# Softmax sums and output tiles of two attention branches: from VectorE and ScalarE to GpSimd

## The chip, the cores and the metric

The kernel runs on one core of one Trainium2 chip. The metric is the device time of one execution in microseconds (us), taken as the median of several runs. The engines are named as in the profile: PE is TensorE (matmul), PEld its weight loads, DVE is VectorE, ACT is ScalarE, POOL is GpSimd, SP is SyncE, which here only issues DMAs.

## The reference, cut to what matters

One layer over 1024 tokens and 256 context tokens, width 1024. Two attention branches of 8 heads (2 key/value heads, head width 64) run on the same input; then they are merged, and a feed-forward layer with a convolution follows. What the change touches is the softmax of the two branches:

```python
def _sink_softmax(scores, sink):                 # first branch (A): window of 128, and the context
    m = jnp.maximum(jnp.max(scores, axis=-1, keepdims=True), sink)
    e = jnp.exp(scores - m)
    return e / (jnp.sum(e, axis=-1, keepdims=True) + jnp.exp(sink - m))
...
p = jax.nn.softmax(_gqa_scores(q_blk, k_all), axis=-1)   # second branch (B): all tokens, and the context
```

## The kernel before, in words

The attention part works in 32 units, in this order: 16 of the first branch (`br` = 0), then 16 of the second (`br` = 1). A unit `br_i_g` is one block `i` of 128 queries and one group `g` of four heads. In the trace the first branch's units run from about 335 to 470 us, the second's to about 760. Names in the trace carry the unit: `sm_4_0` is the tile sm of block 4, group 0 (both branches use the same numbers; the order of time tells them apart).

A unit goes through these steps, and steps of neighbouring units run beside each other:

- `qprep`, two units ahead: POOL casts the unit's queries into `qs` and subtracts to get the low parts (L83 and L86 on `qs`); PE transposes them into `qtr` (four transposes, L483); ACT copies the result, and two DMAs swap its halves. `qs` has one buffer.
- `lat`, once for each head: PE computes scores into `s` (L493, L494, a mask matmul L528), DVE takes their negated maximum into `nm` while it copies them (L538), ACT takes the exponential into `p` and the row sum into `sm` (L505). In the second branch `cxp` does the context's columns first, with sums in `smc` and maxima in `other`.
- `norm`: the tile `f` (128 queries x 4 heads) is a difference of maxima or of maximum and sink; ACT takes its exponential, and it is added to the row sums `sm`. In the second branch POOL also scales the context's `p` by `f`.
- `value_steps`, for the unit before: PE transposes `p` into `ptr` (L614), ACT casts to `pth` (L623), DVE subtracts to `ptl` (L624). For one of the five key tiles in the first branch (two of ten in the second) ACT copies to `prw`, and POOL makes `pth` and `ptl` (pooled tiles). PE multiplies both with the values into `av` (L635, L636).
- `rows`: PE transposes `sm` into `str` (L577), the reciprocal row goes to `rb` by a DMA through memory, which spreads it over all partitions.
- `out_step`: ACT copies `av` to `avs`, POOL copies its upper half to `up`, two adds make the output tile `ot` (L647), POOL multiplies it by `rb` (L650) and splits it into the high and low parts `O` (L83, L86).

All this is written without an order between the engines. A scheduler sets the order of instructions on each engine when the program is built, by its own estimate of what each takes; on the chip each engine's instructions then start in that order, each when what it needs is there. So an edit in one unit can move many instructions of other steps. POOL's queue holds a few more things: in the second branch it casts the weights of the first branch's output product (`hwb`, `lwb`), and it issues the DMAs that add up weight tiles in memory (`sd`).

Of the kernel before, what the change touches and what calls it, by code (L numbers as in the profile page):

```python
# [10 lines left out]
ALU = mybir.AluOpType  # L11
AX = mybir.AxisListType

P = 128
# [54 lines left out]
def layer_kernel(  # L69
# [6 lines left out]
    nc = tc.nc  # L76
    PSUM = bass.MemoryType.PSUM

    def split(src, hi, lo, hi_eng, lo_eng):
        if hi_eng is nc.scalar:  # L80
            nc.scalar.copy(hi, src)  # L81
        elif hi_eng is nc.gpsimd:
            nc.gpsimd.tensor_scalar(out=hi, in0=src, scalar1=1.0, scalar2=0.0, op0=ALU.mult, op1=ALU.add)  # L83
        else:
            hi_eng.tensor_copy(hi, src)
        lo_eng.tensor_tensor(out=lo, in0=src, in1=hi.bitcast(F32), op=ALU.subtract)  # L86
# [8 lines left out]
    def ctile(shape, dt, name):  # L95
        return const.tile(shape, dt, tag=name, name=name)
# [7 lines left out]
    sinkb = ctile([P, 8], F32, "sinkb")  # L104
# [358 lines left out]
    class Unit:  # L463
# [94 lines left out]
        def norm(self):  # L558
            hc = slice(self.g * 4, self.g * 4 + 4)
            f = small(f"f_{self.id}", (P, 4))  # L560
            if self.br:
                nc.vector.tensor_tensor(out=f, in0=self.nm, in1=self.other, op=ALU.subtract)
                nc.scalar.activation(f, f, AF.Exp)
                nc.gpsimd.tensor_tensor(out=self.smc, in0=self.smc, in1=f, op=ALU.mult)
                nc.gpsimd.tensor_tensor(out=self.sm, in0=self.sm, in1=self.smc, op=ALU.add)
                for h in range(4):
                    p = self.pc[h, 1]
                    nc.gpsimd.tensor_scalar(out=p, in0=p, scalar1=f[:, h:h + 1], scalar2=0.0, op0=ALU.mult, op1=ALU.add)
            else:
                nc.vector.tensor_tensor(out=f, in0=self.nm, in1=sinkb[:, hc], op=ALU.add)  # L570
                nc.scalar.activation(f, f, AF.Exp)
                nc.vector.tensor_tensor(out=self.sm, in0=self.sm, in1=f, op=ALU.add)
                nc.vector.reciprocal(self.sm, self.sm)

        def rows(self):
            tr = pt_tile(f"str{self.id}")
            nc.tensor.transpose(tr[0:4, 0:P], self.sm, ident)  # L577
            self.rb = att.tile([P, 2, P], F32, tag="rb", name=f"rb{self.id}", bufs=2)
            row = self.rb[0:4, 0]
            if self.br:  # L580
                nc.vector.reciprocal(row, tr[0:4, 0:P])
            else:
                nc.scalar.copy(row, tr[0:4, 0:P])
            dn = dpool.tile([4, P], F32, tag=f"dn{self.id}", name=f"dn{self.id}")
            tokens.append(f"dn{self.id}")
            nc.sync.dma_start(dn, row)
            for a in range(2):
                nc.sync.dma_start(self.rb[a * HD:(a + 1) * HD],
                                  dn.rearrange("(b a) q -> a b q", a=2)[a].partition_broadcast(HD))
# [15 lines left out]
        def value_steps(self):  # L605
            nm, kt = self.id, self.kt
            vh = self.br * 2 + self.g
            last = self.id == f"1_{NT - 1}_1"
            parts = {}

            def tr_step(n):
                tr = pt_tile(f"ptr{nm}_{n}")
                for h in range(4):
                    nc.tensor.transpose(tr[:, h * P:(h + 1) * P], self.pslice(h, n), ident)  # L614
                hi = att.tile([P, 512], R32, tag="pth", name=f"pth{nm}_{n}", bufs=4)
                lo = att.tile([P, 512], R32, tag="ptl", name=f"ptl{nm}_{n}", bufs=4)
                pooled = n in POOL_LO[self.br] and not last
                if pooled:
                    rw = att.tile([P, 512], F32, tag="ptr", name=f"prw{nm}_{n}", bufs=2)
                    nc.scalar.copy(rw, tr)  # L620
                    split(rw, hi, lo, nc.gpsimd, nc.gpsimd)
                else:
                    nc.scalar.copy(hi, tr)  # L623
                    nc.vector.tensor_tensor(out=lo, in0=tr, in1=hi.bitcast(F32), op=ALU.subtract)  # L624
                parts[n] = hi, lo
                return pooled

            def av_step(n):
                first = self.left == len(kt)
                self.left -= 1  # L630
                if first:
                    self.av = ps2.tile([P, 512], F32, tag="av", name=f"av{nm}")
                hi, lo = parts.pop(n)
                v = VT[kt[n] // 2][:, kt[n] % 2, vh]
                nc.tensor.matmul(self.av, v, hi, start=first, stop=False)  # L635
                nc.tensor.matmul(self.av, v, lo, start=False, stop=self.left == 0)  # L636

            def out_step():
                av = self.av
                avs = att.tile([P, 512], F32, tag="ptr", name=f"avs{nm}", bufs=2)  # L640
                nc.scalar.copy(avs, av)  # L641
                up = att.tile([HD, 512], F32, tag="up", name=f"up{nm}", bufs=1)
                nc.gpsimd.tensor_scalar(out=up, in0=avs[HD:P], scalar1=1.0, scalar2=0.0, op0=ALU.mult, op1=ALU.add)
                ot = att.tile([P, 2, P], F32, tag="ot", name=f"ot{nm}", bufs=1)
                oe = nc.gpsimd if self.br and not last else nc.vector
                for h in range(2):
                    oe.tensor_tensor(out=ot[h * HD:(h + 1) * HD],  # L647
                                     in0=avs[0:HD].rearrange("p (a b q) -> p a b q", b=2, q=P)[:, :, h],
                                     in1=up.rearrange("p (a b q) -> p a b q", b=2, q=P)[:, :, h], op=ALU.add)
                nc.gpsimd.tensor_tensor(out=ot, in0=ot, in1=self.rb, op=ALU.mult)  # L650
                hf = self.i // 4
                qs = slice((self.i % 4) * P, (self.i % 4 + 1) * P)
                split(ot, otile(self.br, hf, 0, self.g)[:, :, qs], otile(self.br, hf, 1, self.g)[:, :, qs],
                      nc.gpsimd, nc.gpsimd)

            def step(ns):
                pooled = [tr_step(n) for n in ns]
                for n, pl in zip(ns, pooled):
                    clk[0] += 1
                    avq.append((self, n, clk[0] + LAG[self.br] + (PLAG[self.br] if pl else 0)))  # L660
                    av_issue()

            self.left = len(kt)
            self.av_step, self.out_step = av_step, out_step
            g = 1 + self.br
            steps = [lambda n=n: step(range(n, n + g)) for n in range(0, len(kt), g)]
            steps.insert(3 if self.br else 2 if self.i else len(steps), self.rows)
            return steps
# [155 lines left out]
    for n, (gi, k) in enumerate(order):  # L824
# [8 lines left out]
        if gi == "g":  # L833
            for hf in (0, 1):
                last = gate(k, hf)
# [50 lines left out]
    def otile(br, hf, hl, g):  # L886
        key = br, hf, hl, g
        if key not in O:
            O[key] = opool.tile([P, 2, HALF], R32, tag="O", name="O%d%d%d%d" % key, bufs=12)
        return O[key]  # L890
# [4 lines left out]
    def pt_tile(name, dt=F32):  # L895
        return ps2.tile([P, 512], dt, tag="pt", name=name, bufs=3)
# [10 lines left out]
    def small(name, shape):  # L907
        return att.tile(list(shape), F32, tag=name.split("_")[0], name=name,
                        bufs=4)
# [4 lines left out]
    def av_issue(flush=False):  # L914
        while avq:
            u = avq[0][0]
            c = [e for e in avq if e[0] is u and (flush or e[2] <= clk[0])]
            if not c:
                return
            e = min(c, key=lambda e: e[2])  # L920
            avq.remove(e)
            u.av_step(e[1])
            if u.left == 0:
                u.out_step()
# [1000 lines left out]
```

## Time and profile before

| what | before |
|---|---|
| median of 3 runs | 1564.17 us (1563.13 to 1565.62) |
| the profiled execution | 1565.22 us, of which 1563.4 us span |
| busy PE / DVE / ACT / POOL | 1531.6 / 1187.6 / 808.6 / 782.2 us |
| granted clock of TensorE, mean | 0.995 |

The span runs from the first to the last instruction; what the time has beyond it lies around the program. A share of busy time is a mean over stages with different limits, so the stages are looked at one by one. A row of the order of time reads: start, duration, engine, line, operation, tiles out<-in, shapes, count, and in brackets how long the engine stood idle before and what ended that.

### The profile page before, as it was taken

Reading aid. Unit: us, or ns where it says so; the run is one execution under the profiler, and the core shown is the slowest. Engines: PE = TensorE matmul, PEld = TensorE weight load, DVE = VectorE, ACT = ScalarE, POOL = GpSimd, SP = SyncE. Lnnn points to the kernel's source line nnn. Section 1 sums busy time; section 2 is a strip of 40 time slices with the busy share of each in tenths; the row PEclk is TensorE's granted clock in tenths of the full one; section 3 lists DMA queues with packets and bytes.
Section 4 is the critical chain, followed back from the end, with each engine's and each line's share of the span. In section 5 each row is a group of like instructions: output and inputs, shape, how many; then the busy total and the mean of one; then the engine's idle time right before and its main releaser. Section 6 shows DMA issues by size and latency. Waiting matters only on the chain.

```text
span 1563.4 us, 22286 instructions
## 1 busy us (share of the span) xinstructions
PE 1531.6 (98%) x7804; PEld 1282.2 (82%) x7804; DVE 1187.6 (76%) x1714; ACT 808.6 (52%) x1431; POOL 782.2 (50%) x795
## 2 busy tenths in 40 slices
PE   9999999999999999999999999999999999999997
PEld 7888888888877877877888997888888888888887
DVE  6677976548887777777774788888888888657884
ACT  5322223358887777777431673544444444435552
POOL 0356422526666777776332455666677764121121
PEclk9999999999999999999999999999999999999998
DMA  9776662322235666631550223233334446996721
GB/s 371 267 239 239 207 245 92 106 84 66 65 116 137 150 149 151 148 80 35 180 184 16 98 79 120 81 112 115 120 102 114 113 117 191 363 265 212 251 103 55
DMA packets 113105, 232.11 MB, mean 148 GB/s; under 512 B 13056, under 2 KB 27904, under 8 KB 112896
## 3 DMA queue, kind: packets, MB, share of 16 engines
q1 hardware_dynamic: 97760, 201.82, 38.4%
q0 software_dynamic: 10400, 20.19, 8.3%
q10 hardware_dynamic: 4832, 8.68, 1.5%
q8 instruction: 61, 1.00, 0.3%
q14 instruction: 52, 0.43, 0.1%
HBM read 179.45 MB, written 65.86 MB: 157 GB/s over the span
## 4 chain that ended last, share of the span: by engine, by line
PE 54%; DVE 3%; ACT 1%; issue 1%; POOL 0%; DVEq 0%; ACTq 0%
PE p L89 4%; PE p L90 4%; PE p L91 4%; PE b L89 2%; PE b L91 2%; PE b L90 2%; PE c L89 2%; PE c L91 2%; PE d L91 2%; PE d L89 2%; PE c L90 2%; PE d L90 2%; PE a L91 2%; PE a L89 2%; PE a L90 2%; PE y L91 2%
## 5 line engine op out<-in xcount | busy, mean ns | idle before, releaser
L624 DVE TENSOR_TENSOR ptl<-ptr,pth 128x512 fp32r<-128x512 f32 x190 | 126.2, 682 | 32.6 <-ACT pth L623 32.2
L623 ACT CAST pth<-ptr 128x512 fp32r<-128x512 f32 x190 | 108.0, 593 | 54.0 <-PE ptr L614 32.6
L86 DVE TENSOR_TENSOR ld<-rd,hd 128x1024 fp32r<-128x1024 f32 x77 | 94.9, 1249 | 50.2 <-ACT hd L81 48.1
L505 ACT ACTIVATE p<-p,nm 128x1024 f32<-128x1024 f32 (+2 forms) x128 | 125.9, 985 | 4.5 <-DVE p L538 4.3
L614 PE MATMUL ptr<-ident,p 128*128 128x128 f32 x816 | 122.4, 277 | 4.4 <-DVE ptl L624 3.2
L81 ACT CAST hd<-rd 128x1024 fp32r<-128x1024 f32 x77 | 79.5, 1050 | 81.1 <-PE p L91 55.1
L614 PEld LDWEIGHTS ptr<-ident,p 128*128 128x128 f32 x816 | 94.1, 141 | 25.6 <-DVE ptl L624 7.9
L86 POOL TENSOR_TENSOR wlg<-wg,whg 128x512 fp32r<-128x512 f32 x32 | 47.7, 1500 | 123.3 <-ACT whg L81 123.3
L635 PE MATMUL av<-pth,VT 128*128 128x512 f32 x236 | 104.6, 443 | 2.1 <-ACT avs L641 1.5
L89 PE MATMUL p<-hd 128*128 128x512 f32 x264 | 103.2, 391 | 0.0
L91 PE MATMUL p<-hd,ld 128*128 128x512 f32 x264 | 102.7, 389 | 0.0
L90 PE MATMUL p<-ld,hd 128*128 128x512 f32 x264 | 102.7, 389 | 0.0
L636 PE MATMUL av<-ptl,VT 128*128 128x512 f32 x236 | 98.1, 416 | 2.7 <-POOL ptl L86 2.7
L89 PE MATMUL g<-hh,whg 128*128 128x512 f32 x256 | 99.9, 390 | 0.0
L91 PE MATMUL g<-hh,wlg 128*128 128x512 f32 x256 | 99.7, 389 | 0.0
L90 PE MATMUL g<-hl,whg 128*128 128x512 f32 x256 | 99.6, 389 | 0.0
L538 DVE TENSOR_SCALAR_CACHE_REDUCE p<-s,cvt,nmc 128x1024 f32<-128x1024 f32 x64 | 83.2, 1316 | 8.8 <-PE s L494 7.7
L493 PE MATMUL s<-KL,q 128*128 128x512 f32 (+2 forms) x192 | 75.6, 394 | 5.3 <-ACT p_x L505 2.8
L787 ACT ACTIVATE sg<-g,bgc 128x512 f32<-128x512 f32 x32 | 22.0, 686 | 96.1 <-PE g L91 96.1
L494 PE MATMUL s<-KL,q 128*128 128x512 f32 (+2 forms) x192 | 71.6, 373 | 0.0
L81 ACT CAST wS<-s 128x512 fp32r<-128x512 f32 x76 | 45.3, 620 | 46.4 <-POOL s L1227 45.7
L81 ACT CAST wA<-ru 128x512 fp32r<-128x512 f32 x57 | 35.5, 623 | 62.4 <-PE d L91 33.8
(436 smaller groups left out, 5015.2 us busy)
## 6 DMA issues: line engine op xcount, KB each, us to landing
wml<-in_wmodT_dram SPq DMA_DIRECT2D x48, 512.0 KB
ru<-in_w_up_dram SPq DMA_DIRECT2D x38, 512.0 KB
rd<-td SPq DMA_DIRECT2D x55, 256.0 KB
rd<-sd SPq DMA_DIRECT2D x44, 256.0 KB
rd<-in_w_dn_dram SPq DMA_DIRECT2D x33, 256.0 KB
wm<-in_wmodT_dram SPq DMA_DIRECT2D x16, 512.0 KB
wg<-in_w_g_dram SPq DMA_DIRECT2D x32, 256.0 KB
sgd<-sg ACTq DMA_DIRECT2D x32, 256.0 KB
```

Source lines behind the costliest of these rows:

```text
L81: nc.scalar.copy(hi, src)
L86: lo_eng.tensor_tensor(out=lo, in0=src, in1=hi.bitcast(F32), op=ALU.subtract)
L89: nc.tensor.matmul(ps, a[0], b[0], start=start, stop=False, skip_group_check=resumed)
L90: nc.tensor.matmul(ps, a[0], b[1], start=False, stop=False, skip_group_check=resumed)
L91: nc.tensor.matmul(ps, a[1], b[0], start=False, stop=stop, skip_group_check=resumed)
L505: nc.scalar.activation(p, s, AF.Exp, bias=nm[:, h:h + 1], scale=scale, accum_out=sm[:, h:h + 1])
L538: nc.vector.tensor_scalar(out=p, in0=o, scalar1=self.qscale(nqs)[:, hs] if self.br else -1.0, scalar2=self.other[:, hs], op0=ALU.mult, op1 ...
L614: nc.tensor.transpose(tr[:, h * P:(h + 1) * P], self.pslice(h, n), ident)
L623: nc.scalar.copy(hi, tr)
L624: nc.vector.tensor_tensor(out=lo, in0=tr, in1=hi.bitcast(F32), op=ALU.subtract)
L635: nc.tensor.matmul(self.av, v, hi, start=first, stop=False)
L636: nc.tensor.matmul(self.av, v, lo, start=False, stop=self.left == 0)
```

## The change

In the first branch the two instructions of `norm` that were on DVE go to POOL, and the reciprocal of `sm` goes: instead `rows` takes the reciprocal of the transposed sums, on DVE and from PSUM, where ACT made a copy before (the second branch did it that way already). The two adds of `out_step` go from DVE to POOL in the first branch too. In the second branch the subtraction that makes `f` goes from DVE to POOL.

```diff
             if self.br:
-                nc.vector.tensor_tensor(out=f, in0=self.nm, in1=self.other, op=ALU.subtract)
+                nc.gpsimd.tensor_tensor(out=f, in0=self.nm, in1=self.other, op=ALU.subtract)
                 nc.scalar.activation(f, f, AF.Exp)
...
             else:
-                nc.vector.tensor_tensor(out=f, in0=self.nm, in1=sinkb[:, hc], op=ALU.add)
+                nc.gpsimd.tensor_tensor(out=f, in0=self.nm, in1=sinkb[:, hc], op=ALU.add)
                 nc.scalar.activation(f, f, AF.Exp)
-                nc.vector.tensor_tensor(out=self.sm, in0=self.sm, in1=f, op=ALU.add)
-                nc.vector.reciprocal(self.sm, self.sm)
+                nc.gpsimd.tensor_tensor(out=self.sm, in0=self.sm, in1=f, op=ALU.add)
...
-            if self.br:
-                nc.vector.reciprocal(row, tr[0:4, 0:P])
-            else:
-                nc.scalar.copy(row, tr[0:4, 0:P])
+            nc.vector.reciprocal(row, tr[0:4, 0:P])
...
-                oe = nc.gpsimd if self.br and not last else nc.vector
+                oe = nc.vector if last else nc.gpsimd
                 for h in range(2):
                     oe.tensor_tensor(out=ot[h * HD:(h + 1) * HD],
```

The scheduler then sets another order. The last number of a tile's name only counts buffers. POOL in the middle of the first branch, from the cast for `qs_5_1` to the one for `qs_6_0`, before:

```order
L83 TENSOR_SCALAR qs_5_1_4221<-Q_4_1588 128x4x64
L643 TENSOR_SCALAR up_3_0_4076<-avs_3_0_4074 64x512
L86 TENSOR_TENSOR qs_5_1_4221<-Q_4_1588,qs_5_1_4221 128x4x64
L83 TENSOR_SCALAR pth_3_1_3_4107<-prw_3_1_3_4109 128x512
L650 TENSOR_TENSOR ot_3_0_4078<-ot_3_0_4078,rb_3_0_3914 128x256
L86 TENSOR_TENSOR ptl_3_1_3_4108<-prw_3_1_3_4109,pth_3_1_3_4107 128x512
L83 TENSOR_SCALAR O_3305<-ot_3_0_4078 128x2x128
L86 TENSOR_TENSOR O_3306<-ot_3_0_4078,O_3305 128x2x128
L83 TENSOR_SCALAR qs_6_0_4355<-Q_6_1591 128x4x64
```

and after (the adds of `out_step` are now L643, its product L646):

```order
L83 TENSOR_SCALAR qs_5_1_4211<-Q_4_1588 128x4x64
L639 TENSOR_SCALAR up_3_0_4068<-avs_3_0_4066 64x512
L86 TENSOR_TENSOR qs_5_1_4211<-Q_4_1588,qs_5_1_4211 128x4x64
L643 TENSOR_TENSOR ot_3_0_4070<-avs_3_0_4066,up_3_0_4068 64x256 x2
L646 TENSOR_TENSOR ot_3_0_4070<-ot_3_0_4070,rb_3_0_3907 128x256
L83 TENSOR_SCALAR O_3302<-ot_3_0_4070 128x2x128
L86 TENSOR_TENSOR O_3303<-ot_3_0_4070,O_3302 128x2x128
L570 TENSOR_TENSOR f_4_0_4076<-nm_4_0_3987,sinkb 128x4
L83 TENSOR_SCALAR pth_3_1_3_4098<-prw_3_1_3_4100 128x512
L86 TENSOR_TENSOR ptl_3_1_3_4099<-prw_3_1_3_4100,pth_3_1_3_4098 128x512
L572 TENSOR_TENSOR sm_4_0_3988<-sm_4_0_3988,f_4_0_4076 128x4
L83 TENSOR_SCALAR qs_6_0_4344<-Q_6_1591 128x4x64
```

The pooled pair `pth`, `ptl` now stands behind the whole output tile, with `f` ahead of it and `sm` behind it, last before the next cast. PE at the same place, from the transpose of the sums to that of the next queries, before:

```order
L577 MATMUL str_4_0_4176<-ident,sm_4_0_3996 4x128
L635 MATMUL av_3_1_4113<-pth_3_1_3_4107,VT_2139 128x512
L614 MATMUL ptr_4_0_2_4193<-ident,p_4_0_0_4014 128x128
L614 MATMUL ptr_4_0_2_4193<-ident,p_4_0_1_4032 128x128
L614 MATMUL ptr_4_0_2_4193<-ident,p_4_0_2_4041 128x128
L614 MATMUL ptr_4_0_2_4193<-ident,p_4_0_3_4058 128x128
L636 MATMUL av_3_1_4113<-ptl_3_1_3_4108,VT_2139 128x512
L635 MATMUL av_3_1_4113<-pth_3_1_4_4121,VT_2139 128x512
L493 MATMUL s_4_1_2_4167<-KL_2131,q_4_1_3965 128x384
L494 MATMUL s_4_1_2_4167<-KL_2131,q_4_1_3966 128x384
```

(the rest of `s_4_1_2`, one product with `ptl_3_1_4` and `qtr_5_1` follow) and after:

```order
L576 MATMUL str_4_0_4167<-ident,sm_4_0_3988 4x128
L631 MATMUL av_3_1_4104<-pth_3_1_3_4098,VT_2139 128x512
L632 MATMUL av_3_1_4104<-ptl_3_1_3_4099,VT_2139 128x512
L610 MATMUL ptr_4_0_2_4184<-ident,p_4_0_0_4006 128x128
L610 MATMUL ptr_4_0_2_4184<-ident,p_4_0_1_4024 128x128
L610 MATMUL ptr_4_0_2_4184<-ident,p_4_0_2_4033 128x128
L610 MATMUL ptr_4_0_2_4184<-ident,p_4_0_3_4050 128x128
L631 MATMUL av_3_1_4104<-pth_3_1_4_4112,VT_2139 128x512
L632 MATMUL av_3_1_4104<-ptl_3_1_4_4113,VT_2139 128x512
L483 MATMUL qtr_5_1_4214<-identr,qs_5_1_4211 128x128 x4
```

The scores `s_4_1_2` have moved ahead of `str_4_0`, and both products of the pooled pair directly behind it. The same order repeats from unit to unit, from the cast for `qs_3_1` to that for the second branch's `qs_0_1`.

In the second branch PE's order stays nearly as it was. POOL at unit 1_1 there, before:

```order
L86 TENSOR_TENSOR ptl_1_0_6_5800<-prw_1_0_6_5801,pth_1_0_6_5799 128x512
L83 TENSOR_SCALAR qs_3_0_6065<-Q_2_547 128x4x64
L86 TENSOR_TENSOR qs_3_0_6065<-Q_2_547,qs_3_0_6065 128x4x64
L564 TENSOR_TENSOR smc_1_1_5640<-smc_1_1_5640,f_1_1_5785 128x4
L568 TENSOR_SCALAR p_1_1_x<-p_1_1_x,f_1_1_5785 128x256
```

and after:

```order
L86 TENSOR_TENSOR ptl_1_0_6_5784<-prw_1_0_6_5785,pth_1_0_6_5783 128x512
L83 TENSOR_SCALAR qs_3_0_6049<-Q_2_547 128x4x64
L86 TENSOR_TENSOR qs_3_0_6049<-Q_2_547,qs_3_0_6049 128x4x64
L562 TENSOR_TENSOR f_1_1_5769<-nm_1_1_5612,nmc_1_1_5623 128x4
L564 TENSOR_TENSOR smc_1_1_5624<-smc_1_1_5624,f_1_1_5769 128x4
```

The subtraction `f_1_1` stands behind the pair on `qs`, directly ahead of its user; ACT's exponential lies between the two. So it is in units 0_1, 2_1, 4_0 and 5_0 as well; in the others `f` follows a `ptl`.

## The prediction

> **What bounds the kernel now.** I read the profile's stages first (the table by stretch), then the waits of TensorE, then the order of time of one unit in the first branch. The table by stretch, for the steady part of the first branch and of the second; the columns are the length, the busy time of PE, PEld, DVE, ACT and POOL, the clock, the DMA share and GB/s:
>
> ```profile
> 365.00:449.00 84.00, 83.17 (x557) 71.14 (x556) 72.82 (x174) 72.49 (x170) 54.96 (x81) 1.00 0.26 72
> 500.00:740.00 240.00, 234.18 (x1349) 192.78 (x1349) 181.90 (x277) 175.72 (x381) 180.26 (x258) 1.00 0.51 120
> ```
>
> PE is busy for 83.2 of 84 us and for 234 of 240: what engines beside PE save is worth at most the little for which PE waits, and what they lose costs only once they make PE wait. POOL, to which the work goes, has 29 us of 84 free in the first branch (55.0 busy), so by shares there is room. Shares don't decide; order does. In the first branch the row qtr, one per unit, is the clock of the loop (order of time, PE):
>
> ```profile
> 365.71 0.46 PE L483 MATMUL qtr<-identr,qs 128*128 128x128 f32 x4
> 374.32 0.46 PE L483 MATMUL qtr<-identr,qs 128*128 128x128 f32 x4
> 448.90 0.46 PE L483 MATMUL qtr<-identr,qs 128*128 128x128 f32 x4
> ```
>
> These are qtr_3_0, qtr_3_1 and, ten units after the first, the second branch's qtr_0_0: 83.19 us, 8.32 us a unit. What PE still waits for in that stretch (who waited for whom: total, times, longest):
>
> ```profile
> PEld ptr L614 <- ACT q L486: 3.0, 10, 0.3
> PEld ptr L614 <- DVE ptl L624: 2.6, 10, 0.4
> ```
>
> 5.6 us of weight-load waits, most of them under a running matmul. POOL, in order of time over one unit:
>
> ```profile
> 374.87 0.41 POOL L83 TENSOR_SCALAR qs<-Q 128x256 fp32r<-128x256 f32 x1 [2.11 <-PE qtr L483]
> 375.36 0.61 POOL L643 TENSOR_SCALAR up<-avs 64x512 f32<-64x512 f32 x1
> 376.06 0.74 POOL L86 TENSOR_TENSOR qs<-Q,qs 128x256 fp32r<-128x256 f32 x1
> 377.84 0.62 POOL L83 TENSOR_SCALAR pth<-prw 128x512 fp32r<-128x512 f32 x1 [1.04 <-ACT prw L620]
> ...
> 383.07 0.40 POOL L83 TENSOR_SCALAR qs<-Q 128x256 fp32r<-128x256 f32 x1 [1.47 <-PE qtr L483]
> ```
>
> The cast of qs starts 0.09 after the end of qtr (374.78), since qs has one buffer. POOL idles 1.5 to 2.1 us there and 1.0 ahead of pth. Nothing that PE needs soon stands at the end of POOL's row: its last two operations are the O splits.
>
> **The change, part by part.** *What leaves DVE and ACT* (groups of instructions in that stretch, then the tile rb):
>
> ```profile
> L647 DVE TENSOR_TENSOR ot<-avs,up 64x256 f32<-64x256 f32 x20 | 8.8, 441 | 0.3 <-POOL up L643 0.2
> L572 DVE TENSOR_TENSOR sm<-sm,f 128x4 f32<-128x4 f32 x10 | 4.7, 468 | 9.0 <-ACT f L571 9.0
> L583 ACT COPY rb<-str x16: 237/254/257, 345.2 to 465.7; 4x128 f32<-4x128 f32 x16
> L581 DVE RECIPROCAL rb<-str x16: 935/941/947, 485.2 to 751.8; 4x128 f32<-4x128 f32 x16
> ```
>
> Per unit DVE loses two adds of 0.44, the sm add of 0.47 with 0.9 of waiting for ACT's exponential ahead of it, and two instructions under 0.2; it gains a reciprocal over 4x128 from PSUM, priced by the second branch's at 0.94. Net some 0.7 busy and 0.9 waiting less. ACT loses its 0.25 copy. Both lie beside PE's 8.3 us: worth 0 here, at most the 5.6 us above. The row-sum DMAs (one write, two broadcasts on SP) now start after a reciprocal of 0.94 instead of a copy of 0.25; the product that needs rb stands more than a unit later in POOL's row, so 0.
>
> *What goes to POOL.* Per unit two adds of 64x256, f and sm. The first branch has no such rows on POOL; the second has the same shapes, in this order:
>
> ```profile
> 500.07 1.52 POOL L647 TENSOR_TENSOR ot<-avs,up 64x256 f32<-64x256 f32 x2
> 501.67 0.73 POOL L650 TENSOR_TENSOR ot<-ot,rb 128x256 f32<-128x256 f32 x1
> 502.49 0.40 POOL L83 TENSOR_SCALAR O<-ot 128x256 fp32r<-128x256 f32 x1
> 502.98 0.73 POOL L86 TENSOR_TENSOR O<-ot,O 128x256 fp32r<-128x256 f32 x1
> 503.68 0.62 POOL L83 TENSOR_SCALAR pth<-prw 128x512 fp32r<-128x512 f32 x1
> 504.38 1.30 POOL L86 TENSOR_TENSOR ptl<-prw,pth 128x512 fp32r<-128x512 f32 x1
> ...
> 507.74 0.20 POOL L564 TENSOR_TENSOR smc<-smc,f 128x4 f32<-128x4 f32 x1
> 508.36 0.20 POOL L565 TENSOR_TENSOR sm<-sm,smc 128x4 f32<-128x4 f32 x1
> ```
>
> That alone fills 1.9 of the 2.9 us that POOL has free a unit. But the new order (the rows under the change) puts sm last on POOL, behind the adds, the rb product, the O splits, f and the pooled pth/ptl; and PE takes str, which reads sm, ahead of the products with that pth/ptl and ahead of qtr. So there is now a ring: qtr ends on PE; POOL casts qs and does its whole row down to sm; PE does str, two av products, four transposes, two av products, qtr; POOL may cast the next qs. In the old order sm is on DVE, and no ring runs through POOL's row.
>
> Its length. POOL: from the cast to the end of the qs subtraction 1.93 (374.87 to 376.80); from the first ot add to the end of ptl 5.61 (500.07 to 505.68); f and sm 0.20 each: 7.94. PE, from rows of the same kind:
>
> ```profile
> 455.98 0.27 PE L577 MATMUL str<-ident,sm 128*4 128x128 f32 x1
> 456.00 0.48 PE L636 MATMUL av<-ptl,VT 128*128 128x512 f32 x1
> 456.32 0.40 PE L635 MATMUL av<-pth,VT 128*128 128x512 f32 x1
> 456.56 0.60 PE L614 MATMUL ptr<-ident,p 128*128 128x128 f32 x4
> 456.91 0.48 PE L636 MATMUL av<-ptl,VT 128*128 128x512 f32 x1
> 457.24 0.54 PE L483 MATMUL qtr<-identr,qs 128*128 128x128 f32 x4
> ```
>
> From str to the end of qtr 1.80, with one av product fewer than the new order has there, which I take at the 0.3 between two starts here: 2.1. Hand-overs: 0.09 to POOL (above), some 0.15 to PE. The ring is 10.2 to 10.3 us against 8.32 a unit. The new order has it from qtr_3_0 to the second branch's qtr_0_0, ten times: (10.25 - 8.32) x 10 = +19. Bounds: without any gaps between instructions (7.46 by durations, PE 1.8) it is 9.3, +9; with 0.25 more, +22. Nothing else in the ring comes later: f needs nm, last written by DVE for s_3, which PE computes right after qtr while POOL has over 5 us of other work; ACT's exponential (0.2) has pth and ptl (1.9) as cover; the pth casts that queue on ACT behind it are due after str.
>
> *The end of the first branch.* Two more rounds of POOL's row, up to ptl_7_0_3 (POOL, then PE):
>
> ```profile
> 463.31 1.27 POOL L86 TENSOR_TENSOR ptl<-prw,pth 128x512 fp32r<-128x512 f32 x1
> 464.63 0.50 PE L636 MATMUL av<-ptl,VT 128*128 128x512 f32 x1 [1.44 <-POOL ptl L86]
> 484.77 1.64 PE L614 MATMUL ptr<-ident,p 128*128 128x128 f32 x8 [1.80 <-DVE ptl L624]
> ```
>
> PE already waits 1.44 for POOL there. From the end of qtr_0_0 (449.36) to that ptl's end (464.58) it is 15.2; two rows of 7.95 and PE's 2.1 between them make 18.0, +2.8. Then ot_7_0 and ot_7_1 (1.6 each) come ahead of later pooled tiles on POOL, beside the two weight-sum DMAs in its queue; the 1.80 of waiting for DVE, itself behind those adds, goes. I take +0.7, together +3.5, bounds 0 and +6. The first units have POOL work to spare: 0, with 1 either way.
>
> *Second branch, f on POOL.* A 0.15 us subtraction leaves DVE, 0.2 comes to POOL, and where the new row has it (after ptl) this costs 0. In units 1_1, 4_0 and 5_0 it stands behind the qs subtraction, directly ahead of smc, while ACT is ready for its exponential earlier (in 0_1 and 2_1, of the same order, POOL is the earlier one) (ACT, then POOL's smc, whose start is about where f could start):
>
> ```profile
> 525.71 0.19 ACT L563 ACTIVATE f<-f 128x4 f32<-128x4 f32 x1
> 618.32 0.19 ACT L563 ACTIVATE f<-f 128x4 f32<-128x4 f32 x1
> 653.62 0.19 ACT L563 ACTIVATE f<-f 128x4 f32<-128x4 f32 x1
> 528.26 0.20 POOL L564 TENSOR_TENSOR smc<-smc,f 128x4 f32<-128x4 f32 x1
> 619.25 0.20 POOL L564 TENSOR_TENSOR smc<-smc,f 128x4 f32<-128x4 f32 x1
> 655.75 0.20 POOL L564 TENSOR_TENSOR smc<-smc,f 128x4 f32<-128x4 f32 x1
> ```
>
> ACT, in order, then stands still 2.6, 0.9 and 2.1 us, plus 0.3 each for f itself, and behind it are three pth casts whose products PE takes within the next us or so. Of these 6.5 us I give PE 4 (less 0.8 of lead each); bounds 0 and +6.5.
>
> Sum: 19 + 3.5 + 4 = +26.5 on the profiled execution's 1565.2 (span 1563.4 and 1.8 around it), so 1591.7; that execution is 1.05 above the median of the three runs, so about 1590.
>
> **Rivals.** *The clock falls in the new gaps.* One row speaks for it, the stretch after the wait of 484.77:
>
> ```profile
> 485.00:490.00 5.00, 5.00 (x28) 4.29 (x27) 4.99 (x9) 3.11 (x5) 4.08 (x6) 0.66 0.19 37
> ```
>
> With PE busy for under half of the 5 us before, the granted clock was 0.66 in these. In the ring PE idles some 2 us in 10, in pieces (for DVE's ptl, for the last exponential, for sm), and PE's 2.1 us of it would take up to 2.1 more: up to +21, the likeliest half of it, 1600. Against it: the 1.44 wait at 464.63 left the clock at 1.0. [...]
>
> *POOL's room is enough: no change.* If PE could pass str and take other ready work, or the ring were under 8.3 us, 7.9 us of POOL in 8.3 would fit: 1564. POOL's operations would have to take 25% less than the rows above; nothing shows that.
>
> *Faster.* The relieved DVE ends PE's waits. This decides only if the ring is shorter than PE's own work; then the 5.6 us above and some of the 1.80 at 484.77 go, of which perhaps 4 reaches the end: 1560.
>
> **How the numbers follow.** The ring as priced 0.79, at 1590 (own range 1577 to 1599, all terms low or high together being unlikely); ring and clock 0.10, 1600 and up; no change 0.06, 1564; faster 0.05, 1560. 0.2% (3 us) is about what this measurement tells from no change. The range 1577 to 1602 leaves out the last two cases and the upper half of the clock's. Faster 0.05, same 0.06, slower 0.89.
>
> **What would show it.** After: qtr 10.2 us apart in the first branch, PE waiting 1 us or more a unit at str for POOL's sm (L572), ten times and the largest of PE's waits there; POOL about 75% busy in that stretch, its only long wait that for qtr; DVE's wait for ACT's f gone; in the second branch ACT waiting for POOL's f in the three units. Wrong if qtr stays under 9 us apart, if POOL's adds beside the first branch's work take other times than 0.73, or if the clock in that stretch is under 1.0.

## The result, and the profile after

The change makes the kernel slower: 1584.97 us median (1584.56 to 1585.69) against 1564.43 us for the kernel before on the same chip, ratio 1.0133 (95% interval 1.0118 to 1.0149), 20.5 us. The prediction was 1590 (1577 to 1602). The profiled execution took 1585.69 us with a span of 1583.9.

The table by stretch, TensorE's waits and the order of time are the views to compare. First the clock of the loop, qtr on PE, after the change: qtr_3_0, 3_1, 4_0, 4_1, and then the second branch's 0_0:

```profile
363.33 0.46 PE L483 MATMUL qtr<-identr,qs 128*128 128x128 f32 x4
374.31 0.67 PE L483 MATMUL qtr<-identr,qs 128*128 128x128 f32 x4
384.40 0.46 PE L483 MATMUL qtr<-identr,qs 128*128 128x128 f32 x4
394.28 0.46 PE L483 MATMUL qtr<-identr,qs 128*128 128x128 f32 x4
...
466.26 0.46 PE L483 MATMUL qtr<-identr,qs 128*128 128x128 f32 x4
```

From qtr_3_0 to the second branch's qtr_0_0 it is 102.93 us; before it was 83.19: **+19.7**. The steady distance is 9.88 us. What PE waits for in that part (who waited for whom: total, times, longest), and GpSimd and PE in order of time over the same unit, cut to the ends of the row and of PE's part:

```profile
PE str L576 <- POOL sm L572: 13.4, 9, 2.2
PE ptr L610 <- DVE ptl L620: 2.0, 1, 2.0
```

```profile
384.95 0.41 POOL L83 TENSOR_SCALAR qs<-Q 128x256 fp32r<-128x256 f32 x1 [2.08 <-PE qtr L483]
...
386.83 1.53 POOL L643 TENSOR_TENSOR ot<-avs,up 64x256 f32<-64x256 f32 x2
...
391.31 1.26 POOL L86 TENSOR_TENSOR ptl<-prw,pth 128x512 fp32r<-128x512 f32 x1
392.53 0.20 POOL L572 TENSOR_TENSOR sm<-sm,f 128x4 f32<-128x4 f32 x1
394.83 0.41 POOL L83 TENSOR_SCALAR qs<-Q 128x256 fp32r<-128x256 f32 x1 [2.10 <-PE qtr L483]
```

```profile
392.79 0.27 PE L576 MATMUL str<-ident,sm 128*4 128x128 f32 x1 [1.48 <-POOL sm L572]
...
394.28 0.46 PE L483 MATMUL qtr<-identr,qs 128*128 128x128 f32 x4
```

The ring of the prediction is there to be read: GpSimd works without a gap from the cast of qs (384.95) to the end of sm (392.73), 7.78 us; PE takes str at once (392.79), and qtr ends 1.95 later (394.74); GpSimd has meanwhile stood still for 2.10, because the next cast needs the buffer that qtr reads. 7.78 + 2.10 = 9.88. Neither engine is full: in a stretch of 66 us (columns as in the prediction) PE is busy for 57.9 (before 66.0), and GpSimd for 47.9 (before 43.5).

```profile
374.00:440.00 66.00, 65.98 (x446) 56.92 (x445) 57.33 (x135) 58.41 (x138) 43.53 (x64) 1.00 0.24 65
374.00:440.00 66.00, 57.93 (x374) 49.47 (x372) 43.13 (x86) 46.46 (x106) 47.88 (x80) 0.98 0.20 49
```

Where the other microseconds are, by the distance between the same instructions in the two traces: up to qtr_3_0 the changed kernel is 2.4 us ahead (363.33 against 365.71); from the second branch's qtr_0_0 to qtr_1_1 it loses 2.3; from there to the end of the attention part 3.5; the rest of the program, which the change does not touch, takes 2.6 less. -2.4 + 19.7 + 2.3 + 3.5 - 2.6 = 20.5. The 3.5 show as the forecast waits of ScalarE for f, and as one that PE did not have before:

```profile
ACT f L563 <- POOL f L562: 5.9, 3, 2.6
PE av L631 <- ACT pth L619: 3.6, 3, 1.5
```

I take the 2.6 for no effect of the change. Before, one piece of 5 us in that part had a granted clock of 0.66 (a loss of 1.7), and one wait of PE for VectorE (L1390 before, L1386 after) was 1.8 instead of 0.6; e7 and e10, two executions of one kernel, differ by 1.1 us from the second branch's qtr_7_1 to their ends.

```profile
850.00:855.00 5.00, 5.00 (x16) 3.92 (x15) 1.69 (x5) 0.00 (x0) 1.03 (x1) 0.66 0.01 3
```

### The profile page after: what moved, and what is told of

Same layout as the page of the kernel before. It is cut to its first block, busy times and chain, and to the rows that moved or that the text cites. A ratio compares the mean times of both kernels' runs of the same rounds, so it can differ in the third digit from the quotient of the medians.

```text
span 1583.9 us, 22300 instructions
## 1 busy us (share of the span) xinstructions
PE 1534.9 (97%) x7804; PEld 1284.7 (81%) x7804; DVE 1172.4 (74%) x1634; ACT 805.1 (51%) x1415; POOL 814.4 (51%) x875
## 4 chain that ended last, share of the span: by engine, by line
PE 53%; DVE 3%; ACT 1%; issue 1%; POOL 1%; DVEq 0%; ACTq 0%; POOLq 0%
PE p L89 4%; PE p L91 4%; PE p L90 4%; PE b L89 2%; PE b L90 2%; PE b L91 2%; PE c L89 2%; PE c L90 2%; PE d L89 2%; PE d L90 2%; PE d L91 2%; PE c L91 2%; PE a L89 2%; PE a L90 2%; PE a L91 2%; PE y L89 2%
## 5 line engine op out<-in xcount | busy, mean ns | idle before, releaser
L493 PE MATMUL s<-KL,q 128*128 128x512 f32 (+2 forms) x192 | 78.3, 408 | 4.2 <-ACT p_x L505 2.8
L494 PE MATMUL s<-KL,q 128*128 128x512 f32 (+2 forms) x192 | 73.2, 381 | 0.0
L538 DVE TENSOR_SCALAR_CACHE_REDUCE p<-s,negsink 128x640 f32<-128x640 f32 (+1 forms) x64 | 51.7, 828 | 24.1 <-PE s L494 23.2
```

Of the source, the lines that this page charges most:

```text
L538: nc.vector.tensor_scalar(out=p, in0=o, scalar1=self.qscale(nqs)[:, hs] if self.br else -1.0, scalar2=self.other[:, hs], op0=ALU.mult, op1 ...
```

## The experiments

Theory: a ring through GpSimd's row. What the change adds there lies between the cast of qs, which waits for PE, and the sums and the pooled pair, for which PE waits. Rivals: GpSimd's load (or its adds beside the other engines' work) as such; sm's place alone; and for the second branch, that its loss came from elsewhere. Each kernel's time stands beside 1563 to 1564 us for the kernel before, timed with it.

**e1, the sums back on VectorE.** PE's order stays word for word that of the changed kernel around str and qtr.

```diff
-                nc.gpsimd.tensor_tensor(out=f, in0=self.nm, in1=sinkb[:, hc], op=ALU.add)
+                nc.vector.tensor_tensor(out=f, in0=self.nm, in1=sinkb[:, hc], op=ALU.add)
...
-                nc.gpsimd.tensor_tensor(out=self.sm, in0=self.sm, in1=f, op=ALU.add)
+                nc.vector.tensor_tensor(out=self.sm, in0=self.sm, in1=f, op=ALU.add)
```

> The changed kernel with the first branch's f and sm back on VectorE; the output adds stay on GpSimd, PE's order is the same as in the changed kernel, and GpSimd's row is the same without f and sm. Ring through the row: GpSimd's row now ends with the pooled ptl, which PE reads just ahead of qtr, so PE waits at av (L632) for ptl instead of at str for sm; cast to the end of ptl 7.62 less 0.16 for f, PE 1.61 from there to the end of qtr, 0.2 of hand-overs: 9.26 us a unit instead of 9.88, 10 units, so 1579 us (1576 to 1582). Rival, only the place of sm last on GpSimd matters: without it nothing holds PE and the period is PE's own 8.3: 1566 to 1569 us. Rival, GpSimd's load (or what its adds do to the others) sets the time: 0.4 of 7.8 us less, 1583 to 1585.

Measured: 1577.46 us, ratio 1.0091 (1.0074 to 1.0108). qtr is 9.33 us apart, and PE's wait has gone to the other instruction, ptl, the pooled low part:

```profile
382.45 0.46 PE L483 MATMUL qtr<-identr,qs 128*128 128x128 f32 x4
391.78 0.46 PE L483 MATMUL qtr<-identr,qs 128*128 128x128 f32 x4
PE av L632 <- POOL ptl L86: 7.9, 10, 0.8
```

So sm's place is not the cause by itself. Whatever PE reads at the end of the row closes the ring.

**e2, the output adds back on VectorE**, f and sm on GpSimd:

```diff
-                oe = nc.vector if last else nc.gpsimd
+                oe = nc.gpsimd if self.br and not last else nc.vector
```

> The changed kernel with the first branch's two output adds back on VectorE; f and sm stay on GpSimd, PE's order around str and qtr is the same. Ring through the row: on GpSimd sm now stands ahead of the rb product and the O splits; cast to the end of sm is 1.9 + 0.2 + 0.7 + 1.2 + 0.2 = 4.2, PE 2.0 and hand-overs 0.2 make 6.4, below PE's 8.2 a unit, so the ring no longer binds: qtr 8.2 to 8.4 us apart, the 14.7 us of waits at str gone, 1585 less 16 to 19: 1566 to 1569 us. Rival, the three engines that f and sm now pass (DVE, GpSimd, ACT, GpSimd, PE) hold PE whatever stands between: str still waits over 1 us a unit and the time stays above 1575.

Measured: 1569.93 us, ratio 1.0041 (1.0026 to 1.0056), 1 us above the band. qtr is 8.29 apart, and of the waits at str one is left:

```profile
PE str L576 <- POOL sm L572: 0.9, 1, 0.9
```

f and sm on GpSimd don't hold PE. What is left over the kernel before is the second branch's f (3.5 from qtr_1_1 to qtr_7_1, about as in the changed kernel) and a wait at the switch between the branches: GpSimd stands 5.8 us at a sum of weights there, which e8 explains.

**e3, the queries prepared earlier**, meant to cut the ring at qtr:

```diff
-                ss.append(units[u + 2].qprep)
+                ss.insert(2 if u + 2 < 16 else len(ss), units[u + 2].qprep)
```

> The changed kernel with one edit: in the first branch the step that prepares the queries is written two heads earlier, so PE takes qtr ahead of str and of the pooled pair; all work that the change moved to GpSimd stays there, and sm still stands last in its row. Ring through the row: the next cast of qs finds qtr done, so the ring is cut; GpSimd's 7.8 us a unit fit into PE's 8.2 to 8.3: no wait for qtr on GpSimd, 1566 to 1570 us. Rival, GpSimd's load or its adds beside the others' work set the time: 1580 or more, with GpSimd still the one that PE waits for at str by over 1 us a unit.

Measured: 1586.64 us, ratio 1.0152 (1.0137 to 1.0167). The expectation of the theory failed. GpSimd no longer waits for qtr, but qtr is still 10.07 us apart, with a new wait in GpSimd's row:

```profile
392.91 0.20 POOL L572 TENSOR_TENSOR sm<-sm,f 128x4 f32<-128x4 f32 x1
393.07 0.40 POOL L83 TENSOR_SCALAR qs<-Q 128x256 fp32r<-128x256 f32 x1
...
396.95 0.61 POOL L639 TENSOR_SCALAR up<-avs 64x512 f32<-64x512 f32 x1 [2.67 <-ACT avs L637]
```

It is a second ring, which I had not seen: up needs avs, ScalarE's copy of av; av's last products stand on PE behind str and the pooled pair; these wait for the end of GpSimd's row, which begins with up. In the changed kernel it is covered by the first. A load without rings would not leave GpSimd standing for 2.67 us a unit, so the rival isn't shown either; that took e9.

**e4, the second branch's f back on VectorE** (one word, in the branch of `if self.br`):

```diff
-                nc.gpsimd.tensor_tensor(out=f, in0=self.nm, in1=self.other, op=ALU.subtract)
+                nc.vector.tensor_tensor(out=f, in0=self.nm, in1=self.other, op=ALU.subtract)
```

> The changed kernel with the second branch's f back on VectorE; the first branch is untouched. If the 3.6 us that the second branch lost come from f behind GpSimd's row: the waits of av for ACT's pth and the 5.9 us of ACT waiting for GpSimd's f go, 1581 to 1582 us. Rival, the second branch lost its 3.6 us to something that was already shifted when it began (other DMA times, output products): 1584 to 1586.

Measured: 1581.75 us, ratio 1.0121 (1.0106 to 1.0136). By the trace the stretch from qtr_1_1 to qtr_7_1 is 219.94 us, as before the change (219.91), instead of 223.54: the 3.6 are f's, and the wait of av for pth is gone. The medians say 2 to 3 us, within their intervals.

**e5, the queries one head earlier:**

```diff
-                ss.append(units[u + 2].qprep)
+                ss.insert(3 if u + 2 < 16 else len(ss), units[u + 2].qprep)
```

> The changed kernel with the first branch's query preparation one head earlier in the program (one less than in e3). All moved work stays on GpSimd; but there the order is now cast, qs subtraction, up, f, pth, output adds, ptl, rb product, sm, O splits, and PE takes qtr right behind str. Two rings, both through GpSimd's row: cast to sm 6.4, PE 0.6, hand-overs 0.2: 7.2 us a unit; and up to sm 5.2, PE from str over av's last product 1.8, the copy to avs 0.9: about 8.0. Both are below PE's 8.2, so if the rings are the cause the time goes back with GpSimd as full as in the changed kernel: qtr 8.2 to 8.5 us apart, 1565 to 1572 us. Rival, 7.8 us of work a unit on GpSimd, or its adds beside the others' work, is the cause: 1580 or more, as in e3.

Measured: 1580.08 us, ratio 1.0109 (1.0095 to 1.0123). A miss, and a flaw of the experiment: I had taken GpSimd's order from one unit, and the next has the old one. Distances alternate between 9.0 and 9.9. In order of time, up waits for avs behind a row in the old order:

```profile
395.40 0.62 POOL L639 TENSOR_SCALAR up<-avs 64x512 f32<-64x512 f32 x1
396.10 1.52 POOL L643 TENSOR_TENSOR ot<-avs,up 64x256 f32<-64x256 f32 x2
...
401.68 0.20 POOL L572 TENSOR_TENSOR sm<-sm,f 128x4 f32<-128x4 f32 x1
...
406.69 0.62 POOL L639 TENSOR_SCALAR up<-avs 64x512 f32<-64x512 f32 x1 [2.85 <-ACT avs L637]
```

**e6, the adds alone**, in the kernel before:

```diff
-                oe = nc.gpsimd if self.br and not last else nc.vector
+                oe = nc.vector if last else nc.gpsimd
```

> The kernel before with only the two output adds of the first branch on GpSimd; f, sm, the reciprocal and the second branch as before. Ring through the row: GpSimd's row from cast to the pooled ptl is that of e1, so 9.3 us a unit and 10 to 12 us more than before: 1574 to 1577 us. Rival, the adds need f and sm behind them to hurt: 1564 to 1567 us.

Measured: 1574.64 us, ratio 1.0072 (1.0058 to 1.0085); qtr 9.33 apart (393.47 to 402.80), PE waiting for ptl as in e1. Two adds of 0.73 were enough here to close a ring that binds.

**e7, the sums alone**, in the kernel before: f, sm and the reciprocal as in the changed kernel, in the first branch only.

```diff
-                nc.vector.tensor_tensor(out=f, in0=self.nm, in1=sinkb[:, hc], op=ALU.add)
+                nc.gpsimd.tensor_tensor(out=f, in0=self.nm, in1=sinkb[:, hc], op=ALU.add)
                 nc.scalar.activation(f, f, AF.Exp)
-                nc.vector.tensor_tensor(out=self.sm, in0=self.sm, in1=f, op=ALU.add)
-                nc.vector.reciprocal(self.sm, self.sm)
+                nc.gpsimd.tensor_tensor(out=self.sm, in0=self.sm, in1=f, op=ALU.add)
...
-            if self.br:
-                nc.vector.reciprocal(row, tr[0:4, 0:P])
-            else:
-                nc.scalar.copy(row, tr[0:4, 0:P])
+            nc.vector.reciprocal(row, tr[0:4, 0:P])
```

> The kernel before with only the first branch's f and sm on GpSimd and the reciprocal from the transposed sums; the adds stay on VectorE, the second branch is as before. Ring 6.4 us, not binding; e2 less the second branch's f, which is worth 3 to 4 us: 1565 to 1568 us. Rival, the second branch's f costs only where the first has moved things: 1569 to 1571 us.

Measured: 1565.3 us, ratio 1.0014 (1.0004 to 1.0023). As forecast; qtr_3_0 is at 364.08, 1.6 ahead of the kernel before.

**e8, the reciprocal alone** (the last piece of e7's edit, and `reciprocal(self.sm, self.sm)` gone; f and sm on VectorE):

> The kernel before with only the reciprocal taken from the transposed sums (on VectorE, 4 x 128, in place of ScalarE's copy); nothing goes to GpSimd. The changed kernel reaches qtr_3_0 2.4 us earlier than the kernel before; if that comes from the first units' sums, which no longer wait for a reciprocal, it shows here alone: 1561 to 1563 us. Rival, VectorE's relief is worth nothing and its longer reciprocal is hidden: 1563 to 1565 us.

Measured: 1570.61 us, ratio 1.0046 (1.0034 to 1.0059): both expectations fell. qtr_3_0 comes at 366.71, 1.0 later than before, so the reciprocal alone does not give the lead at the start. Nor do the adds alone (e6: 365.48, 0.2 ahead). With the reciprocal moved, either group will do: f and sm in e7 (1.6), the adds in e1 (363.23, 2.5). The steady distance is 8.42 us instead of 8.19, with VectorE busier (62.4 of 66 us instead of 57.3; the reciprocal there is 0.94). Most is lost at the switch between the branches, in order of time, GpSimd, VectorE, PE, and then the clock:

```profile
480.55 1.17 POOL L681 DMA_DIRECT2D sd<-in_w_dn_dram  x1 [6.26 <-DMA sd<-in_w_dn_dram]
483.96 0.61 POOL L639 TENSOR_SCALAR up<-avs 64x512 f32<-64x512 f32 x1
484.61 0.85 DVE L643 TENSOR_TENSOR ot<-avs,up 64x256 f32<-64x256 f32 x2 [7.33 <-POOL up L639]
486.24 2.61 PE L610 MATMUL ptr<-ident,p 128*128 128x128 f32 x11 [5.61 <-DVE ptl L620]
485.00:490.00 5.00, 3.77 (x15) 3.47 (x16) 4.69 (x9) 1.86 (x4) 4.06 (x6) 0.50 0.82 150
```

GpSimd issues two sums of weights in memory (sd) there. It stands at the second until a transfer has landed, 13.4 us after it issued the first (467.19); up stands behind that, VectorE's output adds behind up, its other work behind these, PE behind VectorE; and the clock falls to 0.50 on top.

**e9, the output tile behind the sums**, with all of the change's work on GpSimd. The output adds come later in the program, and one added instruction ties the second of them, and so the product and the splits, to the unit's sm:

```diff
+                        nc.gpsimd.tensor_scalar(out=up[:, 0:1], in0=sm[0:HD, 0:1], scalar1=0.0, scalar2=up[:, 0:1],
+                                                op0=ALU.mult, op1=ALU.add)
...
+        while late:
+            late.pop(0)(units[u].sm if u < 16 else None)
```

> The changed kernel with the first branch's output tile tied to the current unit's sm: one element-wide instruction on GpSimd adds 0 times sm to one column of up, so the second output add, the rb product and the O splits can only stand behind sm. All work that the change moved stays on GpSimd, 0.2 us a unit comes on top, PE's order is that of the changed kernel. Ring through the row: cast to the end of sm is 0.5 + 0.7 + 0.7 + 0.8 + 0.2 + 0.7 + 1.2 + 0.2 = 5.0, PE 2.0, hand-overs 0.2: 7.2 us a unit; from up over sm, PE's av, ScalarE's copy and back it is 4.5 + 2.7 = 7.2; GpSimd's whole row is 8.0. All below PE's 8.2 to 8.3, so qtr 8.2 to 8.5 us apart and 1566 to 1571 us, with GpSimd over 90% busy in that stretch. Rival, so much work on GpSimd (or its adds beside the other engines' work) is the cause, wherever it stands: 1580 or more.

Measured: 1566.15 us, ratio 1.0016 (1.0007 to 1.0025), 2.4 us above the kernel before instead of 20.5. GpSimd in order of time, and the stretch of above:

```profile
390.13 0.41 POOL L83 TENSOR_SCALAR qs<-Q 128x256 fp32r<-128x256 f32 x1
...
392.13 0.73 POOL L647 TENSOR_TENSOR ot<-avs,up 64x256 f32<-64x256 f32 x1
...
395.06 0.20 POOL L572 TENSOR_TENSOR sm<-sm,f 128x4 f32<-128x4 f32 x1
...
395.71 0.73 POOL L647 TENSOR_TENSOR ot<-avs,up 64x256 f32<-64x256 f32 x1
...
398.54 0.41 POOL L83 TENSOR_SCALAR qs<-Q 128x256 fp32r<-128x256 f32 x1
374.00:440.00 66.00, 65.85 (x436) 56.53 (x435) 50.36 (x103) 54.90 (x126) 59.32 (x103) 1.00 0.25 65
```

More work on GpSimd than in the changed kernel, no wait in its row, a unit every 8.41 us, and PE busy for 65.9 of 66 us again. The load is not the cause; where it stands in the row is. At 8.41 us a unit, 0.2 above the kernel before, GpSimd (busy for 59.3 of 66 us) has no gap left and most likely sets the distance itself. By the trace the 2.4 us that remain are no loss of the first branch: the second branch's qtr_1_1 comes 0.7 us ahead of the kernel before (486.37 against 487.07), and from there to qtr_7_1 it takes 223.72 instead of 219.91, about f's 3.6 again, as this kernel keeps that edit.

**e10 to e12, the sum of weights moved.** e10 is e7 once more. In e11 and e12 one of the two sums at the switch is issued a unit later, in e7's kernel and in the kernel before:

```diff
             put(1, a(1, 0), a(1, 1))
-            put(3, a(0, 0), a(1, 0))
+            if j0:
+                put(3, a(0, 0), a(1, 0))
+        elif n == -1:
+            put(3, a(0, 0), a(1, 0))
...
+DNS[17] = -1, 0, 4
```

> The kernel of e7 once more, beside e11 and e12 on the same chip: 1564 to 1567 us.

> The kernel of e7 with one of the two weight sums that GpSimd issues at the switch between the branches moved one unit later. In e7 GpSimd stands 4.5 us for the first sum's transfer, ahead of up, and PE then 2.9 us for the copy avs, after which the granted clock is 0.69 for 5 us (1.5 us more). If that stand is what e7 lost, it goes: 1560 to 1562 us, below the kernel before. Rival, the next sum's issue stands for a transfer just as long, or another engine is as late there: 1564 to 1567 us.

> The kernel before with the same weight sum one unit later, nothing else. There GpSimd stands 1.9 us for that transfer, VectorE behind it, PE 1.8 us, and the clock is 0.66 for 5 us (1.7 us more): 1560 to 1562 us if the stand is the cause of PE's wait; 1563 to 1565 if not.

Measured: e10 1565.29 us (one time); e11 **1560.56 us**, ratio 0.9978 (0.9968 to 0.9987); e12 1561.44 us, ratio 0.9982 (0.9972 to 0.9991). Both are as forecast, and faster than both kernels of the change. Their intervals overlap: the gain that they share is the moved transfer, and no further gain of the moved sums is shown. GpSimd's stand for the transfer, in e7, in the kernel before, in e11 and in e12 (in order of time), and then what PE waits for in e7 and e11 from 465 to 500:

```profile
476.73 1.17 POOL L681 DMA_DIRECT2D sd<-in_w_dn_dram  x1 [4.49 <-DMA sd<-in_w_dn_dram]
477.40 1.18 POOL L685 DMA_DIRECT2D sd<-in_w_dn_dram  x1 [1.89 <-DMA sd<-in_w_dn_dram]
472.05 1.38 POOL L682 DMA_DIRECT2D sd<-in_w_dn_dram  x1 [1.90 <-DMA sd<-in_w_dn_dram]
475.99 1.38 POOL L686 DMA_DIRECT2D sd<-in_w_dn_dram  x1
```

```profile
PE av L631 <- ACT avs L637: 2.9, 1, 2.9
PE qtr L484 <- DVE ptl L621: 0.9, 1, 0.9
```

In e11 GpSimd still stands 1.90 at that sum, but PE's longest wait there is the 0.9 above. In e12 the stand is gone, PE's wait for ptl there is 1.1 us instead of 1.8, and the clock behind it stays at 1.00, where it was 0.66 in the kernel before (the row in the prediction; here the 0.66 is the DMA share):

```profile
485.00:490.00 5.00, 5.00 (x38) 4.24 (x36) 5.00 (x9) 4.49 (x10) 3.38 (x6) 1.00 0.66 206
```

The two are 0.7 + 1.7 = 2.4 us, and from the second branch's qtr_1_0 to its qtr_1_1 e12 takes 17.57 us instead of 19.91. So in the traces the gain lies at the switch, and most of it is the clock.

## Why the prediction was right, and where not

*What bounds, and the cost of VectorE's and ScalarE's relief.* Right: VectorE's work in the stretch of 66 us fell from 57.3 to 43.1 and bought nothing there. Wrong by 2.4 at the start, which I had at 0: before, PE waits 2.5 us for VectorE between 330 and 366, 1.1 of it at str for its sm; after, 1.3 for GpSimd's sm. By e1, e6, e7 and e8 the lead needs both, the reciprocal moved and some work off VectorE; neither gives it alone.

*The ring.* The mechanism is the one forecast, and e1, e2, e6 and e9 each move it as its sum says (9.26 forecast and 9.33 measured in e1). The sign "10.2 apart" was 9.88: the terms of 7.94 and 2.3 were 7.78 and 2.10, as GpSimd's instructions follow each other more closely here than in the second branch's rows (sm ends 0.16 behind ptl, not 0.20); the hand-over to PE, an estimate of 0.15, was 0.06 (392.73 to 392.79). Ten times 9.88 is 4.1 less than the 102.93 measured; so +19 against +19.7 is right partly by luck. Half of the 4.1 is the clock: e4, with the same first branch and a clock of 1.00 in the six pieces of 5 us read there, takes 100.87 us for the ten loops (+17.7). The rest lies in three longer loops, the first, one of 10.4 and the last: 10.98, 10.42 and 12.20 here, 10.60, 10.41 and 10.79 in e4. In the last, a statement of the prediction failed, that the pth casts behind f on ScalarE are not due:

```profile
460.33 0.21 ACT L571 ACTIVATE f<-f 128x4 f32<-128x4 f32 x1 [1.94 <-POOL f L570]
461.04 1.29 DVE L620 TENSOR_TENSOR ptl<-ptr,pth 128x512 fp32r<-128x512 f32 x2 [4.20 <-ACT pth L619]
461.79 0.76 PE L610 MATMUL ptr<-ident,p 128*128 128x128 f32 x4 [2.02 <-DVE ptl L620]
```

ScalarE stands 1.94 for GpSimd's f, VectorE's ptl waits for the cast behind it, and PE 2.02 for that: what I had priced in the second branch happened in the first as well, once. And the prediction said that no ring runs through the old row. e6 has a ring with sm on VectorE, through ptl; by the same reading the old order has it too, only shorter than PE's own work.

*The end of the first branch.* +3.5 forecast, +2.3 measured. The 1.80 of waiting for VectorE went, as said; PE waits for the pooled pair instead (3.4 us between 465 and 500).

*Second branch.* +4 forecast, 3.5 measured up to the end of the attention part, 3.6 by e4's trace; the three units and the 5.9 us of ScalarE's wait are those named.

*The sum* was 1591.7 for a profiled execution and that came out at 1585.69: 6.0 too much, of which 2.4 are the start and 2.6 the untouched rest, both taken as 0; the end of the first branch (1.2) and the second branch (0.5) were priced high, and the ring 0.7 low (without the clock's 2.1 it would be 1.3 high). From the end of the attention part on, the same instructions took from 804.2 (e7) to 807.1 us (e8) in these traces, so up to 3 us of such a comparison are the execution's.

*The clock* was given 0.10. One of the prediction's own signs of being wrong was a clock under 1.0 in that stretch, and it came: 0.98 in the 66 us above. In the profiled execution the clock fell behind PE's waits, in four pieces up to qtr_0_1 of the second branch: 5 us x 0.15, 0.19, 0.28 and 0.06 make at most 3.4 us, as PE stood still in part of them. In e4, with the same first branch, it did not fall there; its qtr_0_1 came 2.1 us earlier and its qtr_1_1 3.8. Two pieces of the changed kernel and then the same two of e4:

```profile
370.00:375.00 5.00, 2.81 (x17) 2.18 (x16) 3.95 (x8) 3.46 (x8) 2.31 (x5) 0.85 0.26 70
375.00:380.00 5.00, 5.00 (x27) 4.24 (x28) 1.90 (x4) 3.69 (x9) 4.44 (x8) 0.81 0.25 55
370.00:375.00 5.00, 2.84 (x21) 2.36 (x20) 4.03 (x8) 3.83 (x9) 2.75 (x7) 1.00 0.24 68
375.00:380.00 5.00, 5.00 (x34) 4.25 (x33) 2.53 (x6) 3.19 (x8) 4.59 (x8) 1.00 0.28 60
```

So the rival was half right in kind and small in size (and its row was misread: in the 5 us ahead of 485 PE was busy for 2.58 us, just over half): up to +21 was far off, since a ring's own waits, about 1.5 us in 10, left the clock at 1.00 in every 5 us from 380 to 460. The +21 lets PE's 2.1 us of the ring take twice as long, an estimate that no steady unit shows: at the 0.66 of its row they would take 3.2, and a 0.50 was read in e8, around a wait of 5.6 us.

*No change, and faster*: e9 shows that GpSimd's room does suffice for all of the work, which was the premise of the first of these; it is the order that the scheduler sets which spends it.

## What to carry to other kernels

Before work goes to an engine with room, write down the ring: what its queue waits for first, what others read last from it, and what stands between. Here added work was nearly free in the part of the row that nobody waited for (e9: 8.41 us a unit with all of it, 8.19 before), and between such a wait and such a read it cost what it made the ring longer than the other engine's own work (9.88 us a unit). Look for more than one ring, as cutting the longest left the next in e3 (10.07). And look at the queue of an engine that also issues transfers: GpSimd stood 1.9 us for a transfer in the kernel before and 6.3 in e8, with all that was behind it, and moving the transfer gained 2.3 us in e12, where moving the arithmetic gained none.

## What the runs showed of the hardware

In the 5 us from 370 the changed kernel's PE was busy for 2.81, having waited 2.2 for sm (up to 372.45); the granted clock was 0.85 there and 0.81 in the next 5. In e4 PE was busy for 2.84 of the same 5 us, and the clock was 1.00 in both (rows above). In e8 it was 0.50 in the 5 us in which a wait of 5.6 ended. What sets the clock after a wait, no run here shows.

Some instructions of GpSimd and of VectorE took longer here while one of the other ran. In the kernel before, VectorE's 128x4 add f took 0.16 us while GpSimd stood idle; its 128x4 add sm, of the same shape, began during GpSimd's product, took 0.48, and ended with it (395.57 and 395.54):

```profile
393.96 0.16 DVE L570 TENSOR_TENSOR f<-nm,sinkb 128x4 f32<-128x4 f32 x1
394.81 0.73 POOL L650 TENSOR_TENSOR ot<-ot,rb 128x256 f32<-128x256 f32 x1
395.09 0.48 DVE L572 TENSOR_TENSOR sm<-sm,f 128x4 f32<-128x4 f32 x1 [0.96 <-ACT f L571]
```

It is the same in every steady unit there (sm 0.48, f 0.16). In the second branch f took 0.14 with GpSimd idle (505.97), but 1.18 when it began (471.10) during GpSimd's 128x512 ptl (470.97 to 472.26), and ended with it (472.28). The other way round, GpSimd's 128x512 cast pth took 0.69 instead of 0.62 beside VectorE's two output adds (461.40 to 462.54), which took 1.14 instead of 0.84. Another cast took 0.98 (659.73) while VectorE stood idle, so such a neighbour is not all that lengthens it. In the changed kernel VectorE has no such add left in the steady first branch, and GpSimd's adds took 0.73 there as forecast; so this is not what cost the 20.5 us.
